# A transformer trunk layer: accumulating transfers for the residual, an order for weight sums and for the recurrence's activations

## The chip, the cores and the metric

One core of a Trainium2 chip runs the whole program. The metric is the time of one execution on the device, in microseconds (us); the median of several executions is compared. Five engines work side by side, each through a list of instructions in fixed order: PE (TensorE: matmuls, and their weight loads as PEld), DVE (VectorE), ACT (ScalarE), POOL (GpSimd) and SP (SyncE, which here only issues transfers). They wait for one another by semaphores.

## The reference

One inference step of one trunk layer: x holds 1152 tokens (1024 latent, 128 context), each 1024 wide, in fp32.

```python
def trunk_layer(x, mod, cache, lb, norm_g, ffn1, ffn2, mixer_w):
    m = [mod[:, i][:, None, :] for i in range(N_MOD)]
    x = x + 0.5 * m[2] * swiglu(modulate(x, norm_g[0], m[0], m[1]), *ffn1)
    mix, ctx = token_mixer(modulate(x, norm_g[1], m[3], m[4]), cache, lb, *mixer_w)
    x = x + m[5] * mix
    x = x + 0.5 * m[8] * swiglu(modulate(x, norm_g[2], m[6], m[7]), *ffn2)
    return x, ctx
```

swiglu(h) is (silu(h w1) * (h w3)) w2 with 2816 hidden columns. The token mixer joins an 8-head attention and an 8-head gated linear recurrence in both directions; of the recurrence, what matters here is its end,

```python
    q_h = jax.nn.silu(heads(hq, HG_DK))
    ...
    o_rec = rmsnorm(o_fw + flip(o_bw), hg_norm_g) * jax.nn.silu(heads(hgate, HG_DV))
    ...
    merged = jax.nn.sigmoid(ga) * (o_attn @ w_up_attn) + jax.nn.sigmoid(gr) * (o_rec @ w_up_rec)
```

and a last RMSNorm follows the layer.

## The kernel before

Activations lie transposed: a tile x0 to x7 has 128 of the 1024 channels on its partitions and the 1152 tokens along its columns. Tokens are cut into three chunks of 384 columns in the mixer and four quarters of 288 in the feed-forward networks (FFN). Every fp32 product is three products of split operands: a tile is split into a high part (a rounding copy, on ACT) and a low part (the difference, on DVE or POOL), and PE adds high x high, high x low and low x high. A weight `w` becomes `wh` and `wl` this way in `hl`: with `home="low"` the low part is two DVE operations on 128x512 (L343), without it one POOL operation on 128x1024 (L351).

A scheduler orders each engine's list from the program's order, priorities and an estimate of durations; `keep_in_program_order` pins an instruction.

*Recurrence* (`hgrn`). Heads are worked in four pairs; a loop over heads and chunks weaves the scan (`scan_lev`, `scan_pre`, `scan_out`) with projections that keep PE busy: `proj_f`, `proj_q`, `proj_v`, `proj_gate`, and `proj_sg` for the merge gates. Each projection fills one of two banks "mm"; ACT takes a sigmoid of it (L717, tile sg), and for q (L740) and for the gate (L800) DVE multiplies bank and sigmoid, which frees the bank. When a pair is complete, `proj_gate` also starts its head norm: ACT squares the output oT into osq, `rec_norm` multiplies by ones on PE (tile ops, in a ring of three banks "sm" that the transposes of kt and vt share), `rstd` takes Ln (L429) and Exp (L430) on ACT and a refining step of three operations on DVE, and a fourth scales oT: twelve DVE operations of 128x384 in a pair. Sigmoid lies in one function table of ACT, Ln and Exp in another; a change of table is an ACT_TABLE_LOAD. QP and kr are the queries and keys that the scan scales by its decays before PE multiplies them (lv).

*Second FFN* (`ffn_fast` with l = 1). Three plain blocks of 128 hidden columns (f = 0, 1, 2) run while the norm of the last quarter ends (`norm`, as `self.tail`) and sums of the normalised quarters are made (`sums`: hd, xo; L1718 to L1728). In `norm`, DVE makes xn, ACT its high part bh, POOL its low part bl (L488). xn lies in a ring "sl" of four buffers that the plain blocks' s tiles use too; these leave by transfer (hs<-sl). The other 19 blocks run with seven products in place of eight on 2x2 cut operands; their weights need sums on POOL (ws, raw; L1814, in `fast_ops`) and, for the way down, further sums (wq, L1906 to L1909, in `pair_weights`).

*Fast way down* (`down_fast`). Eight pairs of hidden blocks in groups of 2, 3 and 3; for each group four sweeps m = 0 to 3, each of seven products (`PRODUCTS`, tile d), of which sweep m adds into x[m] and x[m + 4] (L2031) or into the sums su (L2049). In the second FFN the first group overwrites x instead of adding (`first`), and the old x, which lies in memory as xs, is added later: `load_x` transfers it into a spare tile (x<-xs, 576 KB, on SP), and DVE adds it in two halves (L2089). The operands xd of the next group are fetched and split (`down_xs`; low part on POOL, one of a product's blocks on DVE, L2009) during the last sweep of a group: three units behind each product, or two.

Of the kernel before, what the change touches and what calls it, by code (L numbers as in the profile page):

```python
# [9 lines left out]
F32 = mybir.dt.float32  # L10
# [3 lines left out]
AF = mybir.ActivationFunctionType  # L14
# [79 lines left out]
class Trunk:  # L94
# [327 lines left out]
    def rstd(self, r, ps, w=CW, out=None):  # L422
# [6 lines left out]
        nc.scalar.activation(r, ps, AF.Ln, bias=self.epst)  # L429
        nc.scalar.activation(r, r, AF.Exp, scale=-0.5)  # L430
# [18 lines left out]
    def norm(self, c, i):  # L449

        nc = self.nc
        lo, hi = span(c)
        cs = slice(lo, hi)
        rs = self.rs[:, cs]
        if self.mode != "mix":
            rs = self.bank("ps1", "rsp", hi - lo)
        last = self.mode == "mix"
        if last:
            with self.tc.high_priority(offset=600):
                self.stat_end(c, rs)  # L460
        else:
            self.stat_end(c, rs)
        yield
        for k in range(KT):
            t = self.fp.tile([P, hi - lo], F32, tag=self.nt[0], bufs=self.nt[1], name="xn")
# [10 lines left out]
            nc.vector.tensor_mul(t, self.x[k][:, cs], rs)  # L476
# [11 lines left out]
            nc.gpsimd.tensor_sub(tl, t, th)  # L488
            yield

    def place(self, c):
# [222 lines left out]

    def sigm(self, ps):
        s = self.fp.tile([P, CW], F32, tag="sg", bufs=3, name="sg")
        self.nc.scalar.activation(s, ps, AF.Sigmoid)  # L717
        return s

    def proj_f(self, i, h, out):  # L720
# [14 lines left out]
    def proj_q(self, i, out):  # L735
        q = out["q"] = self.tt(F32, "q")
        w = self.load_w(self.a["w_in"][i], KT, P, home="pieces" if i == 2 else "low")
        for c in ORDER:
            ps = yield from self.proj_g(w, c)
            self.nc.vector.tensor_mul(q[:, c * CW : (c + 1) * CW], ps, self.sigm(ps))  # L740
            out["nq"] = out.get("nq", 0) + 1
            yield

# [23 lines left out]
        for f in later:  # L767
            f()

    def proj_gate(self, i, p, pair):  # L770
        nc = self.nc
        oT = pair["o"]
        assert pair["no"] == 4
        w = self.load_w(self.a["w_in"][i], KT, P, home="low")
        sq = self.tt(F32, "osq")[:, :T]
        nc.scalar.activation(sq, oT[:, :T], AF.Square)
        held, normed = [], []

        def norm():
            self.lnexp()  # L780
            for b in ORDER:
                self.rec_norm(b, oT, sq)
            normed.append(1)
            for f in held:
                f()

        def put(cs, s):
# [8 lines left out]
        self.later.append(norm)  # L796
        for c in ORDER:
            ps = yield from self.proj_g(w, c)
            s = self.sigm(ps)
            nc.vector.tensor_mul(s, ps, s)  # L800
            f = partial(put, slice(c * CW, (c + 1) * CW), s)
            if normed:
                f()
            else:
                held.append(f)
            yield
# [8 lines left out]
    def hgrn(self):  # L815
# [10 lines left out]
        self.cnt, self.later = 0, []  # L826
# [21 lines left out]
        def work_of(h):  # L848
            p = h // 2
            work = feed(h + 1) if h + 1 < H else []  # L850
            if h and h % 2 == 0:
                work = work + [sgs.pop(), sgs.pop()] + [self.proj_gate(5 * p - 1, p - 1, pairs[p - 1])]
            while len(work) < 4 - (h == 3) + (h == H - 1):
                work.append(sgs.pop())
            return chain(*work)
# [243 lines left out]
            d["pair"]["no"] = d["pair"].get("no", 0) + 1  # L1099
            yield  # L1100

    def rec_norm(self, c, oT, sq):
        nc = self.nc
        cs = slice(c * CW, (c + 1) * CW)
        ps = self.pp.tile([P, CW], F32, tag="sm", bufs=3, name="ops")
        nc.tensor.matmul(ps, self.onesb, sq[:, cs], start=True, stop=True)
        self.rstd(sq[:, cs], ps)
        nc.vector.scalar_tensor_tensor(oT[:, cs], oT[:, cs], self.hg, sq[:, cs], ALU.mult, ALU.mult)

    def attn(self):  # L1110
# [4 lines left out]
        self.lnexp()  # L1115
# [773 lines left out]

    def pair_weights(self, w2):  # L1890

        nc = self.nc
        self.wsum = self.dp.tile([sum(n for _, n in GROUPS), P, KT // 2, 4, P], F32, name="wsum")
        n = sum(n for _, n in GROUPS)
        for j in range(n):
            f = GROUPS[0][0] + 2 * j
            for m in range(KT // 2 if j < n - GROUPS[-1][1] else 1):
                a, b = [self.fp.tile([P, CW], F32, tag="hf", bufs=self.hfb, name="wq") for _ in range(2)]
                (a11, a21, s1), (s2, a12, a22) = [[t[:, ts(i, P)] for i in range(3)] for t in (a, b)]
                for v, o in enumerate((a11, a21)):  # L1900
                    nc.sync.dma_start(o, w2[f][:, 0, ts(4 * v + m, P)])
                for v, o in enumerate((a12, a22)):
                    nc.sync.dma_start(o, w2[f + 1][:, 0, ts(4 * v + m, P)])
                yield
                yield
                nc.gpsimd.tensor_tensor(s1, a21, a22, ALU.add)  # L1906
# [158 lines left out]
    def down_fast(self, w2, X, xg, ops, made, load_x, load_h, split_h, gm, nxt):  # L2065
# [5 lines left out]
        for g, (f, n) in enumerate(GROUPS):  # L2071
            new = {} if g else X
            last = g == len(GROUPS) - 1
            for m in range(KT // 2):
# [2 lines left out]
                    xg = self.down_xs(g + 1, new)  # L2077
                    next(xg)
                k, raws, xa = 0, [], []
                if g and m in (1, 2):  # L2080
                    xa += [(i, load_x(i)) for i in range(4 * g + 2 * m - 6, 4 * g + 2 * m - 4)]

                def after():
                    nonlocal k
                    if xa and k in (2, 5):
                        i, t = xa.pop(0)
                        for v in range(2):
                            c = ts(v, 2 * QW)
                            self.nc.vector.tensor_add(self.x[i][:, c], t[:, c], self.x[i][:, c])  # L2089
                    if m == KT // 2 - 1 and not last:  # L2090
                        for _ in range(GROUPS[g + 1][1]):
                            next(xg, None)
# [27 lines left out]
    def ffn_fast(self, l, gm, nxt):  # L2120
# [264 lines left out]
```

## Time and profile before

| what | us |
|---|---|
| median of 3 runs | 2859.55 (2859.02 to 2859.63) |
| the profiled execution | 2853.09 |
| its span, from first to last instruction | 2851.2 |
| PE busy in the span | 2767.6 |
| DVE, ACT, POOL busy | 2034.5, 1332.4, 967.3 |

The span's stages, roughly: first FFN to 820 us, recurrence 825 to 1420, attention and merge to 2050, plain blocks of the second FFN to 2122, its fast blocks to 2570, the fast way down to 2759, and the last groups with the final norm to the end. A row of the profile names the line, the engine, the operation, and the output and inputs with their shape; the clock of a stretch is that which the chip granted to PE, 1.00 being full speed. A list of waits tells for each PE instruction that began late which instruction of which engine released it.

### The profile page before, as it was taken

Reading aid. Unit: us, or ns where it says so; the run is one execution under the profiler, and the core shown is the slowest. Engines: PE = TensorE matmul, PEld = TensorE weight load, DVE = VectorE, ACT = ScalarE, POOL = GpSimd, SP = SyncE. Lnnn points to the kernel's source line nnn. Section 1 sums busy time; section 2 is a strip of 40 time slices with the busy share of each in tenths; the row PEclk is TensorE's granted clock in tenths of the full one; section 3 lists DMA queues with packets and bytes.
Section 4 is the critical chain, followed back from the end, with each engine's and each line's share of the span. In section 5 each row is a group of like instructions: output and inputs, shape, how many; then the busy total and the mean of one; then the engine's idle time right before and its main releaser. Section 6 shows DMA issues by size and latency. Waiting matters only on the chain. (4 is left out here: it accounts for less than half of the span.)

```text
span 2851.2 us, 55762 instructions
## 1 busy us (share of the span) xinstructions
PE 2767.6 (97%) x21222; PEld 2637.0 (92%) x21222; DVE 2034.5 (71%) x4430; ACT 1332.4 (47%) x2732; POOL 967.3 (34%) x1004
## 2 busy tenths in 40 slices
PE   8999999999999999999999999899999999999998
PEld 7999999999989998899998778689989999999997
DVE  7867777677678787877356777856766665568875
ACT  6523333321176677667536787731642322235332
POOL 0133232544222222222244454433443443433450
PEclk9999999999999999999999999999999999999999
DMA  6733333743112111112512001273543443347621
GB/s 258 226 129 117 131 124 121 260 171 119 60 68 68 43 62 36 65 50 74 195 61 92 18 16 36 75 246 114 174 142 116 138 159 133 112 154 212 194 100 67
DMA packets 219579, 337.65 MB, mean 118 GB/s; under 512 B 23664, under 2 KB 141360, under 8 KB 219312
## 3 DMA queue, kind: packets, MB, share of 16 engines
q1 hardware_dynamic: 219312, 334.10, 34.9%
q8 instruction: 167, 2.74, 0.4%
q14 instruction: 100, 0.82, 0.1%
HBM read 248.47 MB, written 85.54 MB: 117 GB/s over the span
## 5 line engine op out<-in xcount | busy, mean ns | idle before, releaser
L1844 PE MATMUL b<-xo,wo 128*128 128x288 f32 x3552 | 483.6, 295 | 0.8 <-DVE wo L1819 0.8
L1844 PEld LDWEIGHTS b<-xo,wo 128*128 128x128 f32 x3552 | 475.3, 188 | 1.0 <-DVE wo L1819 1.0
L1844 PE MATMUL b<-bh,wo 128*128 128x288 f32 x1776 | 366.4, 295 | 0.0
L518 PE MATMUL mm<-xh,wh 128*128 128x384 f32 x984 | 345.2, 351 | 11.9 <-DVE sg L800 6.8
L520 PE MATMUL mm<-xh,wl 128*128 128x384 f32 x984 | 334.4, 340 | 0.0
L519 PE MATMUL mm<-xl,wh 128*128 128x384 f32 x984 | 333.7, 339 | 0.0
L547 DVE SCALAR_TENSOR_TENSOR x<-dn,modt,x 128x256 f32<-128x256 f32 (+4 forms) x472 | 226.1, 499 | 89.4 <-PE dn L520 88.0
L1844 PEld LDWEIGHTS b<-bh,wo 128*128 128x128 f32 x1776 | 289.1, 188 | 0.0
L1844 PE MATMUL b<-bl,wo 128*128 128x288 f32 x888 | 262.0, 295 | 0.0
L1818 ACT CAST wo<-raw 128x512 fp32r<-128x512 f32 x185 | 114.8, 621 | 204.0 <-PE b L1844 83.0
L518 PEld LDWEIGHTS mm<-xh,wh 128*128 128x128 f32 x984 | 186.6, 190 | 20.4 <-DVE sg L800 8.2
L2044 PE MATMUL d<-xd,wd 128*128 128x288 f32 x1344 | 181.7, 297 | 9.1 <-DVE x L2031 6.4
L2044 PEld LDWEIGHTS d<-xd,wd 128*128 128x128 f32 x1344 | 180.0, 190 | 10.7 <-ACT wd L1982 3.5
L519 PEld LDWEIGHTS mm<-xl,wh 128*128 128x128 f32 x984 | 186.7, 190 | 1.1 <-issue 0.3
L520 PEld LDWEIGHTS mm<-xh,wl 128*128 128x128 f32 x984 | 186.8, 190 | 0.0
L1819 DVE TENSOR_TENSOR wo<-raw,wo 128x512 fp32r<-128x512 f32 x185 | 127.6, 691 | 71.6 <-ACT wo L1818 69.0
L1541 POOL TENSOR_TENSOR ehl<-e,ehl 128x512 fp32r<-128x512 f32 x93 | 123.9, 1337 | 153.7 <-ACT ehl L1539 85.2
L1844 PEld LDWEIGHTS b<-bl,wo 128*128 128x128 f32 x888 | 167.4, 189 | 0.0
L390 DVE SCALAR_TENSOR_TENSOR junk<-wada,cb 128x512 bf16<-128x512 f32 x224 | 162.3, 724 | 5.8 <-DMA wada<-in_w_aT 4.9
L351 POOL TENSOR_TENSOR wl<-raw,wh 128x1024 fp32r<-128x1024 f32 (+2 forms) x48 | 95.5, 1993 | 159.0 <-ACT wh L350 153.2
L1819 DVE TENSOR_TENSOR wo<-ws,wo 128x512 fp32r<-128x512 f32 x74 | 72.2, 975 | 103.1 <-ACT wo L1818 102.9
L518 PE MATMUL ps<-bh,wh 128*128 128x288 f32 (+1 forms) x448 | 136.4, 305 | 7.4 <-DVE sl L1774 4.1
(458 smaller groups left out, 7118.8 us busy)
## 6 DMA issues: line engine op xcount, KB each, us to landing
raw<-in_w SPq DMA_DIRECT2D x148, 256.0 KB, 3.3
wada<-in_w_aT SPq DMA_DIRECT2D x112, 256.0 KB, 3.0
raw<-in_w SPq DMA_DIRECT2D x42, 512.0 KB, 3.6
raw<-in_w_in SPq DMA_DIRECT2D x41, 512.0 KB, 3.3
xr<-xd SPq DMA_DIRECT2D x56, 288.0 KB, 3.8
hr<-hs SPq DMA_DIRECT2D x26, 576.0 KB, 5.6
hb<-hd SPq DMA_DIRECT2D x44, 288.0 KB, 3.4
hs<-et SPq DMA_DIRECT2D x84, 144.0 KB, 2.2
```

Of the source, the lines that this page charges most:

```text
L351: pin((eng or self.nc.gpsimd).tensor_sub(wl, raw, wh))
L390: nc.vector.scalar_tensor_tensor(junk, ws[n % 2], 1.0, cs[s], ALU.mult, ALU.mult, accum_out=o)
L518: pin(nc.tensor.matmul(ps, wh, xh, start=start and i == 0, stop=False))
L519: pin(nc.tensor.matmul(ps, wh, xl, start=False, stop=False))
L520: pin(nc.tensor.matmul(ps, wl, xh, start=False, stop=stop and i == n - 1))
L547: nc.vector.scalar_tensor_tensor(self.x[m][:, a:b], ps[:, a - lo : b - lo], self.modt[:, gm, m, s : s + 1], self.x[m][:, a:b], ALU.mult, A ...
L1541: eng.tensor_sub(el, e, eh)
L1818: nc.scalar.copy(wh, src[i])
L1819: nc.vector.tensor_sub(wl, src[i], wh)
L1844: nc.tensor.matmul(ps, w[:, k], x[:, k, :QW], start=first, stop=last, skip_group_check=home != i)
L2044: nc.tensor.matmul(ps, w[:, k], xv, start=start, stop=stop, skip_group_check=home != i)
```

## The change

Four places change.

1. In `down_fast` the old x is added by eight transfers issued from POOL that add into x[i] where it lies (L2117 after), in place of eight loads by SP and sixteen DVE adds. The splits of the next group's operands go two behind each product, in the last sweep of a group and in the first of the next.
2. In `pair_weights` the first loads and the first of each four sums are pinned to program order.
3. In the recurrence, order edges without a semaphore (`behind`) put a sigmoid behind the last six Ln and Exp, the table preload behind the last twelve sigmoids, and Ln and Exp behind the preload. The head norm of a pair starts as soon as its outputs are there (`norm_gate`, through `beside`), not with its gate projection. The products of q and of the gate get a higher priority.
4. In the second FFN, the last quarter of the norm takes xn from another ring (six buffers "xp") and makes bl on DVE; the weights of the plain blocks 1 and 2 are split on DVE (`home="low"`).

```diff
+    def behind(self, ins, *first):
+        for f in first:
+            self.tc.add_manual_dep(
+                ins.ins,
+                f.ins.name,
+                mybir.DependencyInfo(mybir.DependencyClass.NoSync, mybir.DependencyReason.DATA),
+                reason="function table",
+            )
+        return ins
+
     def lnexp(self):
-        self.tc.keep_in_program_order(self.nc.scalar.preload_act_table_set("natural_log_exp_and_others"))
...
+        return self.tc.keep_in_program_order(self.nc.scalar.preload_act_table_set("natural_log_exp_and_others"))
...
-        nc.scalar.activation(r, ps, AF.Ln, bias=self.epst)
-        nc.scalar.activation(r, r, AF.Exp, scale=-0.5)
+        pin(nc.scalar.activation(r, ps, AF.Ln, bias=self.epst))
+        pin(nc.scalar.activation(r, r, AF.Exp, scale=-0.5))
...
+            if tail:
+                t = self.half("xn")[:, : hi - lo]
+            else:
+                t = self.fp.tile([P, hi - lo], F32, tag=self.nt[0], bufs=self.nt[1], name="xn")
...
-            nc.gpsimd.tensor_sub(tl, t, th)
+            (nc.vector if tail else nc.gpsimd).tensor_sub(tl, t, th)
...
-        self.nc.scalar.activation(s, ps, AF.Sigmoid)
+        self.sigs.append(self.behind(self.nc.scalar.activation(s, ps, AF.Sigmoid), *self.roots[-6:]))
...
+            s = self.sigm(ps)
+            with self.tc.high_priority(offset=150):
+                self.nc.vector.tensor_mul(q[:, c * CW : (c + 1) * CW], ps, s)
...
+            table = self.behind(self.lnexp(), *self.sigs[-12:])
             for b in ORDER:
-                self.rec_norm(b, oT, sq)
+                self.rec_norm(b, oT, sq, table)
...
+    def beside(self, work, pair):
+        for _ in work:
+            yield
+            if pair["no"] == 4 and "held" not in pair:
+                self.norm_gate(pair)
...
-                work = work + [sgs.pop(), sgs.pop()] + [self.proj_gate(5 * p - 1, p - 1, pairs[p - 1])]
+                work = work + [sgs.pop(), self.beside(sgs.pop(), pairs[p - 1])]
+                work += [self.proj_gate(5 * p - 1, p - 1, pairs[p - 1])]
...
-        self.rstd(sq[:, cs], ps)
+        self.rstd(sq[:, cs], ps, pin=lambda i: self.roots.append(self.behind(i, table)))
...
-                nc.gpsimd.tensor_tensor(s1, a21, a22, ALU.add)
+                pin(nc.gpsimd.tensor_tensor(s1, a21, a22, ALU.add))
...
-                if g and m in (1, 2):
-                    xa += [(i, load_x(i)) for i in range(4 * g + 2 * m - 6, 4 * g + 2 * m - 4)]
+                xa += {(1, 1): (0, 4), (1, 2): (1, 5), (2, 1): (2, 6, 3, 7)}.get((g, m), ())
...
-                    if xa and k in (2, 5):
-                        i, t = xa.pop(0)
-                        for v in range(2):
-                            c = ts(v, 2 * QW)
-                            self.nc.vector.tensor_add(self.x[i][:, c], t[:, c], self.x[i][:, c])
+                    if xa and k in (0, 2, 4, 5):
+                        i = xa.pop(0)
+                        self.nc.gpsimd.dma_start(self.x[i][:, :T], self.xs[i], accum_op=ALU.add)
+                    if m == KT // 2 - 1 and not last or g and not m:
+                        for _ in range(2):
+                            next(xg, None)
...
-            ws = self.pre[f] if l == 0 and f < 2 else [self.load_w(self.a["w13"][l, f, j], KT, P) for j in range(2)]
+            ws = self.pre[f] if l == 0 and f < 2 else [
+                self.load_w(self.a["w13"][l, f, j], KT, P, home="low" if l and f else None) for j in range(2)
+            ]
```

In the order of ACT, the norm of the first pair in the recurrence stood so before (a row is the line, the operation, output and inputs, the shape, and how often in succession):

```order
L429 ACT_TABLE_LOAD
L429 ACTIVATE osq<-ops,epst 128x384 x2
L430 ACT_TABLE_LOAD
L430 ACTIVATE osq<-osq 128x384 x2
L429 ACT_TABLE_LOAD
L429 ACTIVATE osq<-ops,epst 128x384
L717 ACT_TABLE_LOAD
L717 ACTIVATE sg<-mm 128x384
L430 ACT_TABLE_LOAD
L430 ACTIVATE osq<-osq 128x384
L717 ACT_TABLE_LOAD
L717 ACTIVATE sg<-mm 128x384
```

and after the change:

```order
L1094 COPY kT<-kt 128x384
L430 ACT_TABLE_LOAD
L439 ACTIVATE osq<-ops,epst 128x384 x2
L440 ACTIVATE osq<-osq 128x384 x2
L439 ACTIVATE osq<-ops,epst 128x384
L1052 COPY kr_9106<-KE 64x24x8
L440 ACTIVATE osq<-osq 128x384
L730 ACT_TABLE_LOAD
L730 ACTIVATE sg<-mm 128x384
```

Six loads became two, and the block moved up to the copy kT, ahead of the copies kr_9106 and three sigmoids. In the whole program there are 39 table loads before and 21 after.

In POOL's order at the start of the second FFN, from the last quarter but one of the norm on, before:

```order
L488 TENSOR_TENSOR bl<-xn,bh 128x288 x21
L351 TENSOR_TENSOR wl<-raw,wh 128x1024
L488 TENSOR_TENSOR bl<-xn,bh 128x288 x3
L351 TENSOR_TENSOR wl<-raw,wh 128x1024
L1906 TENSOR_TENSOR wq<-wq 128x128
L1907 TENSOR_TENSOR wq<-wq 128x128
L1908 TENSOR_TENSOR wq<-wq 128x128
L1909 TENSOR_TENSOR wq<-wq 128x128
L488 TENSOR_TENSOR bl<-xn,bh 128x288 x5
```

and after:

```order
L501 TENSOR_TENSOR bl<-xn,bh 128x288 x23
L351 TENSOR_TENSOR wl<-raw,wh 128x1024
L501 TENSOR_TENSOR bl<-xn,bh 128x288
L1844 TENSOR_TENSOR ws<-raw 128x256 x2
L1844 TENSOR_TENSOR ws<-ws,raw 128x256 x2
L1844 TENSOR_TENSOR raw<-raw 128x256 x2
L1937 TENSOR_TENSOR wq<-wq 128x128
```

The last eight bl, four weight splits and the first sums wq left this place; POOL comes to the fast blocks' sums ws directly. On DVE they stand there now, between the products sl of the plain blocks:

```order
L1804 TENSOR_TENSOR sl<-ps,sl 128x288
L501 TENSOR_TENSOR bl<-xn,bh 128x288 x2
L343 TENSOR_TENSOR wl<-raw,wh 128x512
L489 TENSOR_TENSOR xn<-x_22049,rsp 128x288
L501 TENSOR_TENSOR bl<-xn,bh 128x288 x2
L489 TENSOR_TENSOR xn<-x_22074,rsp 128x288
L1804 TENSOR_TENSOR sl<-ps,sl 128x288
```

In the second way down POOL's order was, from the first split of operands on:

```order
L2009 TENSOR_TENSOR xd<-xr,xd 128x576 x25
L1977 TENSOR_TENSOR ws<-raw,wr 128x384
L1977 TENSOR_TENSOR raw<-raw 128x384
L2009 TENSOR_TENSOR xd<-xr,xd 128x576 x6
L1977 TENSOR_TENSOR ws<-ws,raw 128x384
L2009 TENSOR_TENSOR xd<-xr,xd 128x576 x4
```

and is now (the number behind x_ is that of the buffer's use; they are x4, x0, x5, x1, x6, x2):

```order
L2040 TENSOR_TENSOR xd<-xr,xd 128x576 x22
L2117 DMA x_29886<-xs 128x1152
L2117 DMA x_29885<-xs 128x1152
L2117 DMA x_30081<-xs 128x1152
L2117 DMA x_30080<-xs 128x1152
L2117 DMA x_30120<-xs 128x1152
L2117 DMA x_30119<-xs 128x1152
L2040 TENSOR_TENSOR xd<-xr,xd 128x576 x3
L2008 TENSOR_TENSOR ws<-raw,wr 128x384
```

Six of the eight transfers stand together behind the 22nd split, which is the first of the last group, and each of them waits for DVE to have written its x; the other two (x7, x3) follow among the last splits.

More of the change, by code (lines that the diff above doesn't have):

```diff
@@ L417, in alloc_h, with rstd @@
         self.xh, self.xl = zip(*hl)
+    def behind(self, ins, *first):
[7 more added lines that the diff above has]
+        return ins
     def lnexp(self):
-        self.tc.keep_in_program_order(self.nc.scalar.preload_act_table_set("natural_log_exp_and_others"))
-    def rstd(self, r, ps, w=CW, out=None):
+        return self.tc.keep_in_program_order(self.nc.scalar.preload_act_table_set("natural_log_exp_and_others"))
+    def rstd(self, r, ps, w=CW, out=None, pin=lambda i: i):
         nc = self.nc
@@ L456, in norm @@
             rs = self.bank("ps1", "rsp", hi - lo)
-        last = self.mode == "mix"
+        last, tail = self.mode == "mix", i == 2 and c == QORDER[-1]
         if last:
@@ L768, in group, with norm_gate @@
             f()
-    def proj_gate(self, i, p, pair):
+    def norm_gate(self, pair):
         nc = self.nc
@@ L773, in proj_gate @@
         assert pair["no"] == 4
-        w = self.load_w(self.a["w_in"][i], KT, P, home="low")
         sq = self.tt(F32, "osq")[:, :T]
         nc.scalar.activation(sq, oT[:, :T], AF.Square)
-        held, normed = [], []
+        held = pair["held"] = []
         def norm():
-            self.lnexp()
+            table = self.behind(self.lnexp(), *self.sigs[-12:])
             for b in ORDER:
-                self.rec_norm(b, oT, sq)
-            normed.append(1)
+                self.rec_norm(b, oT, sq, table)
+            pair["normed"] = 1
             for f in held:
                 f()
+        self.later.append(norm)
+    def beside(self, work, pair):
[3 more added lines that the diff above has]
+                self.norm_gate(pair)
+    def proj_gate(self, i, p, pair):
+        nc = self.nc
+        if "held" not in pair:
+            self.norm_gate(pair)
+        oT, held = pair["o"], pair["held"]
+        w = self.load_w(self.a["w_in"][i], KT, P, home="low")
         def put(cs, s):
@@ L794, in put @@
                 nc.sync.dma_start(self.orec[p, v][:, cs], t.bitcast(F32))
-        self.later.append(norm)
         for c in ORDER:
@@ L799, in proj_gate @@
             s = self.sigm(ps)
-            nc.vector.tensor_mul(s, ps, s)
+            with self.tc.high_priority(offset=150):
+                nc.vector.tensor_mul(s, ps, s)
             f = partial(put, slice(c * CW, (c + 1) * CW), s)
-            if normed:
+            if "normed" in pair:
                 f()
@@ L825, in hgrn @@
         self.A2 = f32("A2", [P, 3, G])
-        self.cnt, self.later = 0, []
+        self.cnt, self.later, self.sigs, self.roots = 0, [], [], []
         heads = [{} for _ in range(H)]
@@ L1100, in scan_out, with rec_norm @@
             yield
-    def rec_norm(self, c, oT, sq):
+    def rec_norm(self, c, oT, sq, table):
         nc = self.nc
@@ L1114, in attn @@
         f32 = lambda n, sh, dt=F32: self.fp.tile(sh, dt, name=n)
-        self.lnexp()
+        self.behind(self.lnexp(), *self.sigs[-12:])
         for tag, n in (("mx", 2), ("av", 2), ("tr", 1)):
@@ L1890, in pair_weights @@
     def pair_weights(self, w2):
-        nc = self.nc
+        nc, pin = self.nc, self.tc.keep_in_program_order
         self.wsum = self.dp.tile([sum(n for _, n in GROUPS), P, KT // 2, 4, P], F32, name="wsum")
@@ L1897, in pair_weights @@
             for m in range(KT // 2 if j < n - GROUPS[-1][1] else 1):
+                load = (lambda i: i) if j or m else pin
                 a, b = [self.fp.tile([P, CW], F32, tag="hf", bufs=self.hfb, name="wq") for _ in range(2)]
@@ L1900, in pair_weights @@
                 for v, o in enumerate((a11, a21)):
-                    nc.sync.dma_start(o, w2[f][:, 0, ts(4 * v + m, P)])
+                    load(nc.sync.dma_start(o, w2[f][:, 0, ts(4 * v + m, P)]))
                 for v, o in enumerate((a12, a22)):
-                    nc.sync.dma_start(o, w2[f + 1][:, 0, ts(4 * v + m, P)])
+                    load(nc.sync.dma_start(o, w2[f + 1][:, 0, ts(4 * v + m, P)]))
                 yield
                 yield
-                nc.gpsimd.tensor_tensor(s1, a21, a22, ALU.add)
+                pin(nc.gpsimd.tensor_tensor(s1, a21, a22, ALU.add))
                 nc.gpsimd.tensor_tensor(s2, s1, a11, ALU.subtract)
@@ L2079, in down_fast @@
                 k, raws, xa = 0, [], []
-                if g and m in (1, 2):
-                    xa += [(i, load_x(i)) for i in range(4 * g + 2 * m - 6, 4 * g + 2 * m - 4)]
+                xa += {(1, 1): (0, 4), (1, 2): (1, 5), (2, 1): (2, 6, 3, 7)}.get((g, m), ())
                 def after():
                     nonlocal k
-                    if xa and k in (2, 5):
-                        i, t = xa.pop(0)
-                        for v in range(2):
-                            c = ts(v, 2 * QW)
-                            self.nc.vector.tensor_add(self.x[i][:, c], t[:, c], self.x[i][:, c])
+                    if xa and k in (0, 2, 4, 5):
[4 more added lines that the diff above has]
+                            next(xg, None)
                     if m == KT // 2 - 1 and not last:
-                        for _ in range(GROUPS[g + 1][1]):
-                            next(xg, None)
+                        pass
                     elif last:
```

2 lines of the change are left out of this document (removed).

## Prediction

> **What bounds the kernel now.** I began with the page: busy shares, then the clock.
>
> ```profile
> span 2851.2 us, 55762 instructions
> PE 2767.6 (97%) x21222; PEld 2637.0 (92%) x21222; DVE 2034.5 (71%) x4430; ACT 1332.4 (47%) x2732; POOL 967.3 (34%) x1004
> ```
>
> PE is busy for 97% of the span, so no edit that leaves the matmuls alone (and this one does) can win more than PE's idle time, 83.6 us, and what PE loses to a lowered clock. Next, the stretches: a row is the window, its length, busy us (and instructions) of PE, PEld, DVE, ACT and POOL, the granted clock, the DMA share and GB/s.
>
> ```profile
> 1050.00:1100.00 50.00, 44.36 (x518) 41.10 (x517) 39.38 (x92) 37.08 (x83) 15.57 (x22) 0.97 0.14 48
> 1200.00:1250.00 50.00, 46.64 (x603) 43.22 (x602) 41.33 (x113) 32.52 (x88) 9.87 (x19) 0.97 0.14 48
> 1300.00:1350.00 50.00, 48.18 (x567) 44.36 (x566) 38.85 (x97) 36.60 (x80) 13.28 (x17) 0.97 0.23 81
> 2100.00:2150.00 50.00, 46.62 (x337) 46.16 (x337) 26.85 (x52) 15.92 (x36) 10.53 (x9) 0.97 0.36 116
> 2300.00:2350.00 50.00, 50.00 (x378) 50.00 (x377) 35.10 (x74) 15.04 (x32) 21.09 (x34) 1.00 0.41 134
> 2700.00:2750.00 50.00, 47.46 (x347) 47.23 (x346) 45.97 (x100) 14.80 (x25) 17.27 (x13) 0.97 0.36 122
> ```
>
> At 2300 PE never waits. It waits in the three places that the diff touches: the recurrence (rows 1 to 3), the start of the second FFN (row 4) and the fast way down (row 6). In all of them the clock reads 0.97: 3% of 50 us, so 1.5 us, is lost on top of each such stall. The list of waits says for whom (total us, times, longest):
>
> ```profile
> PE mm L518 <- DVE sg L800: 6.8, 5, 1.8
> PE d L2044 <- DVE x L2031: 6.4, 5, 2.5
> PE ps L518 <- DVE sl L1774: 4.1, 3, 2.2
> PE lv L1010 <- DVE QP L1047: 3.4, 4, 1.9
> PE mm L518 <- DVE q L740: 3.2, 2, 2.3
> PE ps L519 <- POOL bl L488: 2.2, 4, 1.2
> PE d L2044 <- DVE su L2049: 2.0, 1, 2.0
> ```
>
> **The ceiling.** Recurrence: 6.8 + 3.4 for sg and QP, and three clock rows (4.5), 14.7 us. Start of FFN 2: 4.1 + 2.2 + 1.5 = 7.8 us. Way down: 6.4 + 2.0 + 1.5 = 9.9 us. Together 32.4 us, 1.1%.
>
> **Recurrence.** ScalarE (ACT) normalises a pair of heads like this now (start, us):
>
> ```profile
> 1047.41 1.28 ACT L429 ACT_TABLE_LOAD   x1
> 1048.70 1.06 ACT L429 ACTIVATE osq<-ops,epst 128x384 f32<-128x384 f32 x2
> 1049.78 1.28 ACT L430 ACT_TABLE_LOAD   x1
> 1051.07 0.94 ACT L430 ACTIVATE osq<-osq 128x384 f32<-128x384 f32 x2
> ...
> 1055.22 0.49 ACT L717 ACTIVATE sg<-mm 128x384 f32<-128x384 f32 x1
> 1055.73 1.28 ACT L430 ACT_TABLE_LOAD   x1
> 1057.02 0.52 ACT L430 ACTIVATE osq<-osq 128x384 f32<-128x384 f32 x1
> ```
>
> In this run of activations there are six table loads (three of them shown; 7.7 us), and two sigmoids wait among them; the gate product of DVE (L800) waits for the sigmoid, and PE for the bank that it frees. By the order edges, Ln and Exp of a pair share one stretch between two loads (whole program: 39 loads before, 21 after), and that stretch moves ahead of the gate projections: 2 x 1.28 for loads, some 3.1 us of activations (1.06 + 0.94 + about 0.6 + 0.52), about 6 us with the copy between. PE now takes the three ones-products right behind the kt transposes, in a ring of three banks of which the transposes hold one until ACT has copied it. For such a wait the trace has a price, and for the pair (the second) whose roots already stand together before the change it has another:
>
> ```profile
> PE dS L1072 <- ACT kT L1064: 1.1, 1, 1.1
> PE lv L1010 <- DVE QP L1047: 2.6, 2, 1.9
> PE mm L518 <- DVE sg L800: 1.6, 2, 1.4
> ```
>
> (The last two are of 1150 to 1210 us alone.) That pair pays 2.6 + 1.6, and 1.5 of clock (row 1200): 5.7 us, without a table problem. Its norm puts twelve DVE operations of about 0.5 us in one lump before QP, and the other pairs' norms do the same, only earlier. I therefore take 80% of the sg waits (5.4), half of the QP waits (1.7) and two of three clock losses (3.0), less two new waits of 1.1 in the pairs that move furthest: **7.9, say 8 us**. Ends: 14.7, and, if all four pairs came to cost 5.7, 14.7 - 22.8 = -8. The q products (3.2) stay: raised in priority, they keep their place in DVE's order, and so are not in the sum.
>
> **Start of FFN 2.** The last quarter of the norm waits for buffers that it shares with the plain blocks' s tiles, and POOL holds DVE up:
>
> ```profile
> 2075.49 0.98 DVE L476 TENSOR_TENSOR xn<-x,rsp 128x288 f32<-128x288 f32 x2 [5.14 <-DMA hs<-sl]
> 2106.92 3.36 DVE L1728 TENSOR_TENSOR xo<-hd,xo 128x288 fp32r<-128x288 f32 x3
> 2106.64 2.59 POOL L351 TENSOR_TENSOR wl<-raw,wh 128x1024 fp32r<-128x1024 f32 x1 [10.71 <-ACT wh L350]
> L343 DVE TENSOR_TENSOR wl<-raw,wh x74: 678/691/1403, 859.4 to 1400.1; 128x512 fp32r<-128x512 f32 x74
> ```
>
> The other ring ends the first wait. Three xo operations took 3.36 us beside POOL's 2.59 us weight split; at the 0.49 each of the first row (the same shape) they would take 1.5. Moving splits to DVE adds 8 x 0.49 + 8 x 0.69 = 9.4 us there, in a stretch where DVE stands at 26.85 of 50 (row 2100): room enough, and POOL's blocks go. What is late next is the sums (hd, xo), which now stand behind the weight splits and are due when the fast products begin at about 2122. I take bl's 2.2, the two shorter sl waits (4.1 - 2.2 = 1.9) and half of the longest with its clock (3.7 / 2): **6 us**. Ends: 7.8, and -2.2 if bl's four waits return as waits for DVE with as much again for the sums and nothing else goes.
>
> **Way down.** Before: eight loads, sixteen DVE adds. After: eight accumulating transfers issued by POOL.
>
> ```profile
> L2089 DVE TENSOR_TENSOR x<-x,x x16: 742/752/1127, 2634.9 to 2734.0; 128x576 f32<-128x576 f32 x16
> DMA x<-xs: 6.3, 2
> L2009 POOL TENSOR_TENSOR xd<-xr,xd x35: 1420/1750/1964, 2550.5 to 2695.8; 128x576 fp32r<-128x576 f32 x35
> 2670.93 5.05 POOL L2009 TENSOR_TENSOR xd<-xr,xd 128x576 fp32r<-128x576 f32 x3 [12.84 <-ACT xd L2008]
> 2690.78 6.74 POOL L2009 TENSOR_TENSOR xd<-xr,xd 128x576 fp32r<-128x576 f32 x4
> L1906 POOL TENSOR_TENSOR wq<-wq x23: 453/462/919, 2070.0 to 2473.4; 128x128 f32<-128x128 f32 x23
> L2191 POOL TENSOR_TENSOR hl<-hr,hh x26: 2667/2696/2748, 522.4 to 2765.7; 128x1152 fp32r<-128x1152 f32 x26
> L2044 PE MATMUL d<-xd,wd x1344: 288/295/442, 2568.3 to 2758.8; 128*128 128x288 f32 x192
> x<-xs SPq DMA_DIRECT2D x16, 576.0 KB, 6.5
> xd<-et SPq DMA_DIRECT2D x16, 576.0 KB, 3.5
> ```
>
> DVE (45.97 of 50 at 2700) sheds 16 x 0.75 = 12 us of adds and 6.3 us of waiting for loads. The splits of one group (21) now run over two sweeps instead of one, so POOL and DVE collide less: POOL's took 1.75 in the median against 1.42 at best. What stays: as many splits, and DVE's other work. I take two thirds of the ceiling, 6.5 us; the upper end is 9.9.
>
> The new price is POOL's. In its queue six transfers stand between the first split of the last group and the next three. In the trace these splits run from 2670.93 to 2690.78 + 6.74 = 2697.5. PE needs the last one at the last product of that group's first sweep: 1344 products of 132 ns (50 us / 378) are 177.4 us, eight equal shares of 22.2; groups of 2, 3 and 3 blocks in four sweeps make 16.6 us a sweep of the last group, and the last group starts 66.6 us and 6 us of waits (2.5 + 2.0 + 1.5) before 2758.8, at 2686, so its first sweep's last product begins at 2686 + 6/7 x 16.6 + 2.0 (the wait for su) = 2702.5. Slack: 5 us. One issue on POOL is not in the trace. Bounds: 0.46 us, POOL's smallest operation (L1906), and 2.70, one of the transfer's own width (L2191): 2.8 to 16.2 us for six, a loss of 0 to 11. An issue moves no elements itself, so it is nearer the small one: I take 1.0, six in 6 us, a loss of 1. Way down: **5.5 us**; ends 9.9 and -11.
>
> **Sum.** 8 + 6 + 5.5 = 19.5 us of the profiled 2853.09 (span 2851.2, 1.9 around it): 2833.6. The median of the runs shown, 2859.55, is 6.5 above that execution; the saving carries over: **2840 us**.
>
> **Rivals.**
> (a) *POOL is held by its transfers.* For it: the queue order, and POOL and DVE plainly stretching each other. Against: slack and small issues. At 2.7 us each 11 us are lost, and of the way down's gain only the earlier group's half, 3, stays: 2859.55 - 14 - 3 + 11 = 2853.5; at half that loss, 2848. The Trainium skill, page "SBUF — State Buffer", section "A bandwidth-pool intuition that's wrong (but worth ruling out)", says that a transfer issued from GpSimd took about 3.1 us instead of 0.62 beside a DVE copy, as DVE locks GpSimd out of the port through which it writes descriptors; six would be 18.6 us and the loss 13.6, so 2856 as an estimate from that page, against 2853.5 by the largest POOL row. Of the lock the trace shows as much as that POOL's splits go from 1.42 to 1.75 us; an issue beside DVE no run so far shows.
> (b) *The norm's lump.* All pairs pay 5.7 us: recurrence -8, so 2859.55 + 8 - 11.5 = 2856, within what can be told from no change.
> (c) *Everything goes*: 2859.55 - 32.4 = 2827.
> (d) *Accumulation is slow: slower than before.* The transfers go out from about 2672 and are needed, in DVE's in-order queue, from the third product of the last group on, the eighth by its last sweep at about 2745: eight in 73 us, 9 us each if they pass one after another. Beyond, DVE stops and PE with it. If an accumulation, which must also read what it adds to, takes twice the plain 6.5, that is 8 x 13 - 72 = 32 us late: 2859.55 - 14 + 32 = 2878. It decides from 72 + 14 = 86 us, 10.8 us each. Against: as many bytes landed in 3.5 us in the other row, doubled 7. The page "DMA: Bandwidth & Descriptors" of the Trainium skill, section "Anatomy of one DMA — SWDGE (gpsimd) path", has 2.0 us plus bytes over 436 GB/s, an estimate of 3.4 us here, far from the point; no run shows it yet for an accumulation.
>
> **Numbers.** Chances: forecast 0.62, (a) 0.17, (b) 0.08, (c) 0.08, (d) 0.05. About 0.2%, 5.7 us, can be told from no change. Faster: 0.62 + 0.08 + 0.12 of (a); same: (b) and the rest of (a), 0.13; slower: (d). The range takes in (c) and most of (a) and (b), and leaves (d) out: 2827 to 2857.
>
> **What would show it.** Right: 21 table loads; sg L800 under 2 us in the waits of PE; DVE's wait for hs<-sl gone and bl L488 without a wait; window 2700 at clock 1.00 and DVE below 43. Wrong: waits of lv for QP above 5 us or new ones for kT (b); splits of the last group ending later than 2702 on POOL, with PE's d waiting for them (a); DVE's L2031 waiting for transfers (d). The prediction falls if these lists shrink while idle of the same size appears at other rows, since PE's order is nearly unchanged.

## The result, and the profile after

| | us |
|---|---|
| before, median of 4 runs | 2859.38 (2859.02 to 2859.63) |
| after, median of 4 runs | 2839.01 (2837.92 to 2844.36) |
| ratio | 0.9933 (95%: 0.9918 to 0.9949) |
| profiled executions, before and after | 2853.09, 2839.99 |

The change is faster by 0.7%. The two profiled executions differ by 13.1 us, the medians by 20.4: the four runs of before shown here lie above most of its runs. In the experiments below before has medians of 2855.35 (20 runs), 2854.95 (9) and 2855.54 (21), from 2848.7 to 2860.1, and the whole change 2838.51 and 2839.80; the saving there is 16 us. Two executions of a later kernel (the early norm without edges), of 3243 and 6431 us, lie far outside the rest and are left out of its ratio.

PE's list of waits of the changed kernel, the rows that answer to those shown of before, or that come ahead of them now:

```profile
PE mm L531 <- DVE q L755: 4.4, 3, 2.4
PE lv L1040 <- DVE QP L1077: 4.0, 4, 1.4
PE d L2075 <- DVE su L2080: 3.9, 1, 3.9
PE d L2075 <- DVE x L2062: 3.7, 3, 1.8
PE ops L1136 <- ACT kT L1094: 1.7, 2, 0.9
PE mm L531 <- DVE sg L829: 1.3, 3, 0.7
```

The wait for sg fell from 6.8 to 1.3; those of the second FFN's start (sl 4.1, bl 2.2) are gone from the list. QP and q did not shrink, kT's is the new one that was foreseen, and su doubled (2.0 to 3.9). The stretches, with the columns of before:

```profile
1050.00:1100.00 50.00, 45.59 (x533) 42.25 (x532) 41.22 (x98) 32.25 (x86) 15.29 (x22) 1.00 0.20 62
2100.00:2150.00 50.00, 50.00 (x380) 50.00 (x379) 27.82 (x55) 15.05 (x32) 17.48 (x22) 1.00 0.40 127
2650.00:2700.00 50.00, 44.24 (x312) 43.80 (x311) 43.07 (x70) 20.15 (x36) 32.22 (x24) 0.93 0.73 192
2700.00:2750.00 50.00, 50.00 (x371) 50.00 (x370) 39.78 (x84) 18.86 (x27) 26.21 (x16) 1.00 0.36 119
```

At 2100 PE never waits any more. In the way down the last stretch is clean, but the one before it has PE at 44.24 and the clock at 0.93. Lengths by stage, from one start of an instruction to another (the first vt to the last nps of onesk; the last product with mh or ml to the first d; the first d to the last):

| us | before | after | after, again (two profiles) |
|---|---|---|---|
| recurrence | 593.5 | 588.8 | 587.1, 588.1 |
| second FFN, from w_out to the way down | 512.0 | 501.4 | 502.5, 502.1 |
| fast way down | 190.5 | 189.8 | 190.6, 191.2 |

In the other profiles the recurrence lasts 593 to 595 us with before's code and 587 to 588 with the changed code, the second FFN 513 to 515 and 502 to 504 us. So the gain lies in the first two stages. In the way down sixteen additions of DVE (12 us) left, and nothing came of it. The place is here, on DVE and on POOL (start, us):

```profile
2675.45 1.45 DVE L2040 TENSOR_TENSOR xd<-xr,xd 128x576 fp32r<-128x576 f32 x1 [0.47 <-ACT xd L2039]
2676.82 1.76 DVE L2014 TENSOR_TENSOR wd<-wr,wd 128x384 fp32r<-128x384 f32 x1
2678.51 0.93 DVE L2062 SCALAR_TENSOR_TENSOR x<-d,modt,x 128x288 f32<-128x288 f32 x2
2679.36 5.37 DVE L2040 TENSOR_TENSOR xd<-xr,xd 128x576 fp32r<-128x576 f32 x1
2684.65 0.55 DVE L2014 TENSOR_TENSOR wd<-wr,wd 128x384 fp32r<-128x384 f32 x1
```

```profile
2676.25 1.92 POOL L2040 TENSOR_TENSOR xd<-xr,xd 128x576 fp32r<-128x576 f32 x1
2678.11 0.87 POOL L2117 DMA_DIRECT2D x<-xs  x1
2678.72 3.11 POOL L2040 TENSOR_TENSOR xd<-xr,xd 128x576 fp32r<-128x576 f32 x2
2681.47 1.20 POOL L2117 DMA_DIRECT2D x<-xs  x1
2682.09 2.02 POOL L2040 TENSOR_TENSOR xd<-xr,xd 128x576 fp32r<-128x576 f32 x1
```

A split of 0.74 us at best took 5.37 on DVE. It began 0.4 us after the first of two issues (x7) had ended on POOL, beside the two splits that stand between the issues, and ended (2684.73) only after POOL's last split (2684.11). PE's wait of 3.9 us for su follows, then 6.8 us at half clock (2684 to 2692), which cost 3.4, so some 7 us in all.

### The profile page after: what moved, and what is told of

It reads as the page before. It is cut to its first block, busy times and chain, and to the rows that moved or that the text cites. A ratio compares the mean times of both kernels' runs of the same rounds, so it can differ in the third digit from the quotient of the medians.

```text
span 2837.9 us, 55729 instructions
## 1 busy us (share of the span) xinstructions
PE 2764.2 (97%) x21222; PEld 2635.3 (93%) x21222; DVE 2027.6 (71%) x4430; ACT 1309.7 (46%) x2714; POOL 952.7 (34%) x1000
## 5 line engine op out<-in xcount | busy, mean ns | idle before, releaser
L1844 POOL TENSOR_TENSOR ws<-raw 128x256 f32<-128x256 f32 x74 | 64.5, 893 | 282.3 <-DMA raw<-in_w 211.7
## 6 DMA issues: line engine op xcount, KB each, us to landing
raw<-in_w SPq DMA_DIRECT2D x42, 512.0 KB, 3.7
raw<-in_w_in SPq DMA_DIRECT2D x41, 512.0 KB, 3.5
```

The source lines that it names most:

```text
L1844: nc.gpsimd.tensor_tensor(o[:, c], x[:, c], y[:, c], op)
```

## The experiments

**Parts alone.** Three kernels are before with one part of the diff each, all else as it was; a fourth adds the pins of the weight sums to the part at the start of the second FFN.

The recurrence's part (order edges, early head norm, priorities):

```diff
+            if pair["no"] == 4 and "held" not in pair:
+                self.norm_gate(pair)
...
+        self.sigs.append(self.behind(self.nc.scalar.activation(s, ps, AF.Sigmoid), *self.roots[-6:]))
```

> Before with the recurrence's part alone (order edges, early head norm, priorities). If the parts add up as the two profiles have them, the recurrence ends about 5 us earlier (the last product nps L1264 ended at 1456.9 before, 1453.3 after, and 1.1 us of the difference was lost ahead of the recurrence), and the median falls by 4 to 6 us; by the prediction's term it falls by 8. Rival: the median of the whole change (20.4 us) is larger than the difference of the two profiled executions (13.1) because this part gains more in unprofiled executions; then it falls by 10 or more.

Measured: 2847.43 against 2855.35, ratio 0.9967 (0.9955 to 0.9980), so 9 us (6 to 13); recurrence 586.9 us. The term of 8 holds; the stage itself is shorter by 6.6 to 7.9 us than in profiles with before's code (593.5 to 594.8).

The second FFN's start, without the pinned sums:

```diff
+                t = self.half("xn")[:, : hi - lo]
...
+            (nc.vector if tail else nc.gpsimd).tensor_sub(tl, t, th)
...
+                self.load_w(self.a["w13"][l, f, j], KT, P, home="low" if l and f else None) for j in range(2)
```

> Before with the part at the start of the second FFN alone (own ring and DVE for the last quarter of the norm, weight splits on DVE). By the profiles PE's waits of 2076 to 2122 us (8.0 us) and the clock loss behind them (1.7) go: the median falls by 8 to 10 us. By the prediction's term 6. Rival: the pinned weight sums are what clears POOL there, and without them the splits of DVE still collide with the sums wq: then it falls by 5 or less and waits of PE for sl or bl stay above 2 us in the window.

Measured: 2848.84, ratio 0.9977 (0.9968 to 0.9986), 7 us; the stage lasts 506.5, not 501 to 503. In its profile, POOL's work just before the fast blocks, and then PE's wait for sl in that stretch:

```profile
2109.36 0.49 POOL L1909 TENSOR_TENSOR wq<-wq 128x128 f32<-128x128 f32 x1 [9.12 <-DMA wq<-in_w]
2109.93 3.24 POOL L1910 TENSOR_TENSOR wq<-wq 128x128 f32<-128x128 f32 x1
2113.13 1.13 POOL L1911 TENSOR_TENSOR wq<-wq 128x128 f32<-128x128 f32 x1
2114.22 0.46 POOL L1912 TENSOR_TENSOR wq<-wq 128x128 f32<-128x128 f32 x1
2114.64 1.65 POOL L1817 TENSOR_TENSOR ws<-raw 128x256 f32<-128x256 f32 x2
```

```profile
PE ps L521 <- DVE sl L1777: 2.0, 1, 2.0
```

The sums wq (0.46 us each at best) still stand ahead of ws; one took 3.24 beside DVE, which made hd and xo without a gap then. The rival that asked for the pins was right in part: more than half of the gain comes without them. The next kernel adds them, for the sums and for the first loads:

```diff
+                pin(nc.gpsimd.tensor_tensor(s1, a21, a22, ALU.add))
```

> Before with the part at the start of the second FFN and the pinned weight sums together. With the first part alone the stretch from the last product of w_out to the first of the way down fell from 512 to 506.5 us, in the whole change to 501.4, and a wait for sl (2.0) with its lowered clock at 2121 us stayed. Theory: the pins account for the rest, since POOL's sums wq no longer come ahead of the fast blocks' first sums: the stretch lasts 501 to 503 us and the median falls 3 to 5 us below that of the first part alone (2848.8). Rival: the pins do nothing, the stretch stays at 505 to 508.

Measured: 2844.66 (before on that chip 2854.95), ratio 0.9961 (0.9949 to 0.9974), 11 us; the stage lasts 503.1. ws starts 6 us sooner, 4 of them within the stage (which itself began 2 us sooner), and the wait is down to 0.2:

```profile
2108.49 2.90 POOL L1817 TENSOR_TENSOR ws<-raw 128x256 f32<-128x256 f32 x2 [42.01 <-DVE xo L1731]
```

```profile
PE ps L521 <- DVE sl L1777: 0.2, 1, 0.2
```

The way down's part:

```diff
+                        self.nc.gpsimd.dma_start(self.x[i][:, :T], self.xs[i], accum_op=ALU.add)
+                    if m == KT // 2 - 1 and not last or g and not m:
```

> Before with the way down's part alone (accumulating transfers and spread splits). By the profiles the way down lasts 190.5 us before and 189.7 after: the median changes by less than 2 us, since the waits for x that go (6.4 to 3.7) return as one for su (3.9) and a longer clock loss. By the prediction's term it falls by 5.5. Rival: the wait for su in the profile is a chance of that execution; then the median falls by 5 to 8 and the profile of this run has no DVE split above 2.5 us.

Measured: 2857.19, ratio 1.0000 (0.9991 to 1.0009); the way down lasts 190.4 us, with a wait for su of 4.9. No gain: the interval leaves room for 2.6 us at most, and the long DVE operation was there again (5.79 us). The other way round, the whole change without this part:

> The whole change without its part in the way down (eight loads and sixteen DVE adds as before, splits three by three). Theory: that part gained nothing, as the wait for su and the lowered clock behind the long DVE split took back what the adds gave; then this kernel is within 2 us of the whole change, and its way down lasts 188 to 191 us. By the prediction's term it would be 5.5 us slower.

Measured: 2836.45, ratio to before 0.9938 (0.9925 to 0.9952), beside 2838.51 and 0.9944 (0.9931 to 0.9956) of the whole change on the same chip; the way down lasts 187.6 us against 190.6. The term of 5.5 is refuted. The part loses a little, if anything: the medians differ by 2 us, within their intervals.

**The long DVE operation.** Only the place of two transfers on POOL changes (they go out at 2706 and 2711 us now, among sums of weights); the other engines' orders around it stay the same.

```diff
-                xa += {(1, 1): (0, 4), (1, 2): (1, 5), (2, 1): (2, 6, 3, 7)}.get((g, m), ())
+                xa += {(1, 1): (0, 4), (1, 2): (1, 5), (2, 1): (2, 6), (2, 2): (3, 7)}.get((g, m), ())
...
-                        self.nc.gpsimd.dma_start(self.x[i][:, :T], self.xs[i], accum_op=ALU.add)
+                        t = self.nc.gpsimd.dma_start(self.x[i][:, :T], self.xs[i], accum_op=ALU.add)
+                        if i in (3, 7):
+                            self.tc.keep_in_program_order(t)
```

> After with the last two accumulating transfers (x7, x3) issued behind the last group's splits on POOL instead of among them; nothing else moves on any engine. Theory: the two issues among gapless splits on POOL keep DVE's own split from its turn (5.37 us instead of 0.75 to 1.8) and so cause the wait for su (3.9) and 3.4 us of lowered clock: this kernel is 4 to 7 us faster than the whole change (median about 2833), with no DVE split above 2.5 us and a wait for su under 2. Rival: POOL's splits alone do it, the issues are short (0.87); then the long split and the wait stay, and the median is within 2 us of 2839.

Measured: 2835.00, ratio 0.9923 (0.9910 to 0.9937); the way down lasts 187.2 us, its wait for su is 1.8, and no DVE operation takes over 2.5 us. The whole change beside other kernels, for comparison:

> The whole change once more, beside the three kernels below on one chip. The first result compared four runs with four of before (2859.4); on another chip before ran from 2850 to 2860 with a median of 2855.4. Expected: 2836 to 2842, some 15 to 18 us below the median of before. Its profile should show the DVE split of over 4 us beside the transfers x7 and x3 again, since that comes from the order on POOL and not from chance. Rival (chance): no DVE split above 2.5 us and a wait for su under 2.

Measured: 2838.51. The wait for su was 4.4, and the long operation was there, this time one that splits a weight, not xd:

```profile
2676.77 5.78 DVE L2014 TENSOR_TENSOR wd<-wr,wd 128x384 fp32r<-128x384 f32 x1
```

It is whichever operation DVE starts behind the first issue. Then both versions on one chip:

> The version with the transfers x7 and x3 behind the splits, once more, beside the whole change on one chip: 3 to 6 us below it; no DVE operation above 2.5 us in the way down, which lasts 186 to 189 us. If the difference is under 1.5 us, the long DVE operation is hidden elsewhere.

> The whole change, for the comparison with the kernel before this one: 2836 to 2842 us; in its way down one DVE operation of over 4 us, from the issue of x7 to the end of POOL's last split, whichever operation it is (a split of xd in one profile, one of wd in the next), and the way down lasts 189 to 191 us.

Measured: 2836.97, ratio 0.9932 (0.9919 to 0.9944), against 2839.80, 0.9940 (0.9926 to 0.9953). The difference, 2.8 us, is just short of what I expected, and the intervals overlap. In the stage it is plain: 187.1 us against 191.2, a wait for su of 2.3 against 5.1. POOL's last four splits in the two profiles, first with the transfers behind them,

```profile
2675.25 6.69 POOL L2040 TENSOR_TENSOR xd<-xr,xd 128x576 fp32r<-128x576 f32 x4
```

then, in the whole change, with the transfers among them, and DVE's operation beside these:

```profile
2677.95 1.75 POOL L2040 TENSOR_TENSOR xd<-xr,xd 128x576 fp32r<-128x576 f32 x1
2679.65 0.86 POOL L2117 DMA_DIRECT2D x<-xs  x1
2680.26 3.06 POOL L2040 TENSOR_TENSOR xd<-xr,xd 128x576 fp32r<-128x576 f32 x2
2683.00 1.18 POOL L2117 DMA_DIRECT2D x<-xs  x1
2683.61 1.99 POOL L2040 TENSOR_TENSOR xd<-xr,xd 128x576 fp32r<-128x576 f32 x1
```

```profile
2680.44 5.79 DVE L2040 TENSOR_TENSOR xd<-xr,xd 128x576 fp32r<-128x576 f32 x1 [1.18 <-ACT xd L2039]
```

Four splits in a row let DVE in between (its operations take 1.5 to 1.8 us there); the same four with issues between them hold it for the rest of the burst. In all five profiles with this burst the long operation ended 0.4 us (wd) or 0.6 us (xd) behind POOL's last split. Alone it takes 0.54 or 0.74, so nearly all of its length is waiting.

**The spread.** The whole change with the splits three by three, in a group's last sweep:

```diff
-                    if m == KT // 2 - 1 and not last or g and not m:
-                        for _ in range(2):
-                            next(xg, None)
                     if m == KT // 2 - 1 and not last:
-                        pass
+                        for _ in range(GROUPS[g + 1][1]):
+                            next(xg, None)
```

> The whole change with the accumulating transfers but the splits three by three in the last sweep of a group, as before. Theory of the prediction: the spread relieves DVE and POOL at the ends of the groups; without it the waits for x at about 2600 to 2620 us (1.9 in the profile of the whole change) grow to 3 or more, and the median rises by 1 to 4 us. Rival: the order that the scheduler makes of it is nearly the same (a dozen rows of POOL differ), so it is within 1 us.

Measured: 2840.79, ratio 0.9947 (0.9935 to 0.9960), against 0.9944 of the whole change. The medians differ by 2.3 us, well within their intervals, and the way down lasts 192.2 us against 189.8 to 191.2: this doesn't show that the spread is worth anything. The waits for x are 3.2 us in the way down, against 2.9 to 4.7 in three profiles of the whole change, and the long DVE operation is there (5.78, a wait for su of 5.6).

**Edges or place.** Before with the order edges and priorities, the head norm left with the gate projection; then with the early norm and no edges.

```diff
-                work = work + [sgs.pop(), self.beside(sgs.pop(), pairs[p - 1])]
+                work = work + [sgs.pop(), sgs.pop()]
```

> Before with the recurrence's order edges and priorities, but the head norm where it was, with the gate projection: 21 table loads, the norm's place as before. With the whole part the recurrence (from the first transpose of v to the last product nps) lasted 586.9 us, before 593.5 to 594.8. Theory: the table loads are the cause of the waits for the gate's sigmoid, so the edges alone bring most of it: 587 to 590 us, sg waits under 3 us in all, and a median 5 to 8 us below before. Rival: the place is what matters (the norm's twelve DVE operations and its stretch on ACT fall into the gate projection): 591 us or more, and waits for sg of 5 us or more stay.

```diff
-        for f in first:
+        for f in ():
```

> Before with the early head norm and priorities but no order edges: 37 table loads, the norm ahead of the gate projection. Theory (table loads): the waits move with the norm to other sigmoids of the recurrence, and it lasts 591 us or more. Rival (place): 587 to 590 us, since the gate's products no longer queue behind the norm on DVE.

Measured: edges alone 0.9984 of before (0.9975 to 0.9993), 5 us, recurrence 589.4 us, the wait for sg 5.5 in all (I had expected under 3); early norm alone 0.9987 (0.9978 to 0.9997), 4 us, 593.1 us, sg 3.7. First the edges, then the early norm:

```profile
PE mm L528 <- DVE sg L826: 5.5, 6, 1.4
```

```profile
PE mm L528 <- DVE sg L826: 3.7, 3, 1.8
```

By the stage the edges bring the larger part of the gain (one profile each); the medians don't tell the two apart. With the norm beside the gate's products these still wait, table loads or not; only both together (586.9 us) bring sg down to 1.4. All three kernels have the raised priorities, whose share was not tried.

## Why the prediction was right, and where it was not

The time and the sign were right, but that the time came within 1 us is in part luck: 8 + 6 + 5.5 was 9, 11 and 0 by the ratios of the parts (each to 3 or 4 us), so errors cancelled, and against later runs of before the whole is worth 16 rather than 19.5.

*Recurrence, 8.* Right in its mechanism. ACT's norm of the first pair after the change, as foreseen two loads and some 6 us:

```profile
1037.94 0.48 ACT L1094 COPY kT<-kt 128x384 f32<-128x384 f32 x1
1038.44 1.28 ACT L430 ACT_TABLE_LOAD   x1
1039.73 1.05 ACT L439 ACTIVATE osq<-ops,epst 128x384 f32<-128x384 f32 x2
1040.68 0.94 ACT L440 ACTIVATE osq<-osq 128x384 f32<-128x384 f32 x2
...
1042.76 1.28 ACT L730 ACT_TABLE_LOAD   x1
1044.05 0.49 ACT L730 ACTIVATE sg<-mm 128x384 f32<-128x384 f32 x1
```

Of its terms: sg, 5.4 foreseen, 5.5 gone (6.8 to 1.3); the new waits for kT, 2.2 foreseen, 1.7. Wrong was QP: half of 3.4 was foreseen gone; it is 4.0, and 3.1 to 3.7 in other profiles of the changed recurrence. That q stays (3.2 foreseen, 4.4 measured) is not refuted, as three other profiles with before's recurrence have 3.5 to 4.4. The clock's 3.0 was no term of its own: two other profiles with before's recurrence show one half-clock spell in it instead of four, and it lasted 593.7 and 594.8 us all the same, with sg waits of 9.0 and 9.3 instead of 6.8. Whoever adds waits and clock losses of one profile thus counts in part the same time twice; the likely reason, which no run isolates, is that the other engines catch up while PE is slow. The rival of the norm's lump, -8, is refuted.

*Start of FFN 2, 6.* The mechanism was right: no wait for hs<-sl on DVE, none of PE for bl or sl in the profile after (in other profiles of the same code up to 1.5 us for sl). The size was not. Without the pins the part is worth 7 us, near the 6; but I put the pinned sums down at nothing, without a word. They clear POOL just there and are worth some 4 us, which the order of POOL, quoted in the section on the change, showed already. The stage shows it (506.5 to 503.1); the two ratios, 0.9977 and 0.9961, have intervals that overlap. Nor was the ceiling of 7.8 one: the stage shortened by 10.6 us in the profiles before and after. The waits listed there (sl, bl and 0.4 for bh) and 1.7 of clock come to 8.4 us; where the rest lies no row here tells.

*Way down, 5.5.* Wrong. The step that failed is "In its queue six transfers stand between the first split of the last group and the next three": the order was so, but the place in time was not. The splits of that group did not run from 2670.93 in the trace before, as I read it. The first stood 14 us ahead of the next three, and POOL was idle on both sides of it:

```profile
2656.49 1.60 POOL L2009 TENSOR_TENSOR xd<-xr,xd 128x576 fp32r<-128x576 f32 x1 [28.69 <-ACT xd L2008]
```

After the change it came at 2618, and the six transfers went out when POOL was idle:

```profile
2618.34 1.44 POOL L2040 TENSOR_TENSOR xd<-xr,xd 128x576 fp32r<-128x576 f32 x1 [3.31 <-ACT xd L2039]
2622.60 1.02 POOL L2117 DMA_DIRECT2D x<-xs  x1 [2.82 <-DVE x L2062]
...
2654.29 0.86 POOL L2117 DMA_DIRECT2D x<-xs  x1 [1.52 <-DVE x L2062]
2655.82 5.06 POOL L2040 TENSOR_TENSOR xd<-xr,xd 128x576 fp32r<-128x576 f32 x3 [0.67 <-ACT xd L2039]
```

An issue costs POOL 0.86 to 1.20 us, as taken (1.0), and POOL's last split ended at 2684, ahead of its date: 2702.5 in before is 2690 here, since the way down starts 12.5 us sooner. Rival (a) looked at POOL held by its transfers; what happened is the reverse, DVE held by POOL, at the other two transfers, which I had not weighed at all. The second step that failed is "two thirds of the ceiling": without the long operation (the version with late transfers) the way down lasts 187.1 and 187.2 us, and with before's code 187.6 to 190.5 in seven profiles, so that twelve microseconds less of DVE are worth 2 us of PE on average, and at the least 0.4. The sign set for the window at 2700 (clock 1.00, DVE below 43) came true and shows little: that row holds later work now, and the place of before's last stalls, 2694 to 2716, lies at 2682 to 2703 here, mostly in the row at 2650 with its clock of 0.93. Rival (d) is refuted: the transfers landed in 6.0 to 9.7 us, and nothing waited for them.

The version with late transfers has the lowest ratios to before of all that ran, 0.9923 and 0.9932, though their intervals overlap with those of the whole change.

## What to carry to other kernels

A place in an engine's order is not a place in time: date a moved instruction by what it waits for before pricing what stands behind it. Keep issues of transfers out of a gapless burst on POOL while DVE is due; behind the burst they cost nothing here. And price each edit by itself, those that only pin an order too.

## What the runs showed of the hardware

DVE can be held by POOL over several of its instructions: 5.37 to 5.79 us for operations of 0.54 or 0.74, once in each of the five profiles with two issues among POOL's last splits, against at most 2.5 in both with the issues behind them. Which arbiter does it, no run shows. The Trainium skill, page "SBUF — State Buffer", section "A bandwidth-pool intuition that's wrong (but worth ruling out)", tells of the other direction: a transfer issued from GpSimd took 3.1 us instead of 0.62, as DVE, in a copy, kept GpSimd from writing its descriptors. No run here shows that: no issue took over 1.20 us beside a DVE at work for 43 of 50 us, though with other operations than a copy.

An accumulating transfer of 576 KB landed 7.9 us (median of 8) after its issue; eight plain ones of the same tensor and size, earlier in the same profile, took 7.5 in the median. So here accumulation cost little, and the 3.4 us estimated in rival (d) was too low.

The lowered clock is in part a draw: the wait of about 2.5 us for x in before's way down was followed by 3.4 us at half clock in the profile of before, and by none in that of the whole change without its way down. The Trainium skill, page "TensorE: Matmul & The Clock Gate", section "What's actually happening", says that the window of 3.4 us in which activity is watched runs freely, so that it depends on the moment what falls into it; that agrees with these two, which is as far as the runs go.
